# Expert gathers in float32 from one normed copy, one buffer of gathered tokens, a ring of 22 matrix buffers

## The chip, the core and the metric

The kernel runs on one core of a Trainium2 chip. TensorE (PE) multiplies matrices and loads their weights (PEld in the profile), VectorE (DVE), ScalarE (ACT) and GpSimd (POOL) do the elementwise work, and SyncE (SP) issues nearly all transfers from HBM to the on-chip memory, which 16 DMA engines carry out. Each engine has a queue of its own and runs it in order. The metric is the device time of one execution in microseconds. [...]

## The reference

Two transformer blocks are computed one after the other, on 256 tokens of 1024 features, in float32. The first has an attention mixer and a mixture of experts; the second a recurrent mixer and a dense feed-forward part. The change concerns the mixture of experts in the first block:

```python
def hierarchical_moe(h, w_group, b_group, w_router, b_router, w_gate, w_up, w_down):
    t = h.reshape(-1, d)
    g_logits = t @ w_group + b_group                 # 4 groups of 8 experts
    g_sel = jnp.argmax(g_logits, axis=-1)
    ...
    top_v, top_i = lax.top_k(e_logits, TOPK_EXPERT)  # 2 experts of the chosen group
    w_top = jax.nn.softmax(top_v, axis=-1) * p_group[:, None]
    comb = jnp.sum(jax.nn.one_hot(eid, N_EXPERTS) * w_top[..., None], axis=1)
    hg = jnp.einsum('nd,edf->nef', t, w_gate)        # 32 experts, 1024 x 256
    hu = jnp.einsum('nd,edf->nef', t, w_up)
    a = jax.nn.silu(hg) * hu * comb[:, :, None]
    y = jnp.einsum('nef,efd->nd', a, w_down)         # 32 experts, 256 x 1024
```

Each token goes to 2 of 32 experts. Three matrices of 1 MB belong to each expert, 96 MB in all, and each is read from HBM once.

## The kernel before

The experts are taken in 8 units of 4. A unit gives each of its experts 32 slots; a one-hot matrix tells which token sits in which slot. The unit's work on PE is, in the order of the loop at the end of the code below: gate product (`gate_up(st, "g")`, tile p_gu from the matrices eg), up product (p_gu from eu), then, for the next unit, `prepare`, which builds the one-hot matrix on DVE (`onehot`, tile Pq) and gathers that unit's tokens into its slots (`gather`: p_xg, moved into the tile xg by ACT and DVE, which also apply the norm's scale and shift), then `slots` (p_pw, the transposed one-hot matrix, and p_cs, each slot's weight in the mixture), `turn` (p_at, the activations transposed), `down` (p_dn from the matrices ed) and `scatter` (p_sc, which adds the result to the tokens).

The normed tokens are kept as three bf16 parts that add up to the float32 value (`xn3`, made by `cut3`; the trace calls them xn); so a gather is 3 parts x 2 token tiles x 8 feature tiles = 48 bf16 matmuls with a bf16 one-hot matrix. Unit 0's gather runs before the parts are there and is in float32 already (`gather_t`, tile P). The mixture weights are split in three bf16 columns too (`comb3`).

If an expert has more tokens than 32, the unit has a second set of slots. Ahead of units 1 to 6 stands `branch(st)`, a conditional block that does the whole unit again for the slots behind the 32nd, with a one-hot matrix and a gather of its own. Whether it runs is decided on the chip, by a count that each engine loads. For this input the block of unit 3 runs and the other five are skipped. The code of the block lies in the instruction stream in any case, and a skipped block is a jump. A hint for the branch stands on PE's queue, behind the `turn` of the unit before (`mark_branch_hint_location`). In unit 2's block there is also a fallback for counts above 64.

The expert matrices come through a ring of buffers of 1 MB in three pools (`RING`, `AGAIN`; pool 1 raw, 2 raw2, 3 raw3). `load_experts(n)` puts the next n loads on SP's queue: first 16, in front of the router 4 more, then 4 behind the gate, 4 (5 in unit 0) behind the up and 4 behind the down product of each unit. The fifth buffer of raw3 first holds the normed tokens in float32 (`xn2`) and serves as a buffer for matrices from then on, so that the first round of the ring has 20 places and each later one 21. A load waits until the matrix that its buffer held has been used. The instruction queues are put in order by a scheduler, from the order of the code, what each instruction depends on, and the calls that keep the order of the program.

There are two buffers for gathered tokens (`XGB = 2`), so that a second-slot unit gathers into one while the other keeps the tokens of the unit itself, which were gathered before the branch.

Of the kernel before, what the change touches and what calls it, by code (L numbers as in the profile page):

```python
# [17 lines left out]
D = 1024  # L18
# [3 lines left out]
SLOTS = 32  # L22
NEXP = 32
YF = 2
XGB = 2
RAW1 = 11
HALVES = ((0, 512), (512, 512))
LAST = ((0,512),(512,384),(896,128))


RING = [1, 1, 2, 2, 1, 1, 1, 1, 1, 2, 1, 1, 2, 2, 1, 1, 3, 3, 3, 3]
AGAIN = RING[:4] + [3] + RING[4:]


@with_exitstack
def tile_block(ctx: ExitStack, tc: tile.TileContext, A, out):
    nc = tc.nc
    pe, act, dve, pool = nc.tensor, nc.scalar, nc.vector, nc.gpsimd
# [10 lines left out]
    def bank(shape, name):  # L49
        return ps.tile(shape, FT, name=name, tag="bank")  # L50
# [51 lines left out]
    def mm(o, lhsT, rhs, start, stop):  # L102
        held_pe(pe.matmul(o, lhsT, rhs, start=start, stop=stop, skip_group_check=True))  # L103
# [127 lines left out]
    def load_experts(n):  # L231

        for _ in range(n):
            if not loads:
                return
            i = len(W)
            e, k = loads.pop(0)
            name = {"g": "w_gate", "u": "w_up", "d": "w_down"}[k]
            shape = (2, D) if k == "d" else (8, 256)
            n = RING[i] if i < len(RING) else AGAIN[(i - len(RING)) % len(AGAIN)]  # L240
            pool_, tag = (raw, "raw") if n == 1 else (raw2, "raw2") if n == 2 else (raw3, "raw3")
            t = pool_.tile([128, RAW], FT, name=f"e{k}", tag=tag)
# [13 lines left out]
            W[e, k] = v  # L256
# [631 lines left out]
    for c in "iiqikqqFqXFXbbYYbbvYTXXF22XY2XYvvYXYXv2BWBa2aaBYBnB3BC33CCCC3BCanB3C!CR4D45D45D45EH45DDDEoHEoEoDEoDEEESZpppp":  # L888
# [8 lines left out]
        else:  # L897
# [9 lines left out]


    m1 = p2.enter_context(tc.tile_pool(name="m1", bufs=1, side="right", reuse_waits="tile"))
    raw3 = p2.enter_context(tc.tile_pool(name="raw3", bufs=AGAIN.count(3), side="right", reuse_waits="tile"))  # L910

    xn2 = raw3.tile([128, RAW], FT, name="xn2", tag="raw3").rearrange("p (t d) -> p t d", t=2)
    tc.keep_in_program_order(pool.memset(xn2[:, 0, 0:1], 0.0))
    load_experts(RING.count(3))

    lg = m1.tile([128, 2, 36], FT, name="lg")
    le32 = m1.tile([128, 2, NEXP], FT, name="le32", tag="le32")
    iota1 = m1.tile([128, 2 * SLOTS], FT, name="iota1")
# [10 lines left out]
    gfi = m1.tile([128, 2], FT, name="gfi")  # L929
    top = m1.tile([128, 2, 8], FT, name="top")  # L930

    xn3 = m1.tile([128, 3, 2, 8, 128], BF, name="xn3")
    xh = [m1.tile([128, 8, 128], FT, name="h2", tag="xg", bufs=XGB).rearrange("p (a j) n -> p a j n", a=2),
          [m1.tile([128, 4, 128], FT, name="h2", tag="yf", bufs=YF) for _ in range(2)]]
    xh[0] = [xh[0][:, 0], xh[0][:, 1]]
    P0 = m1.tile([128, 2, 4, SLOTS], FT, name="P0", tag="sl")
    pos_ = bank([128, 2, NEXP], "p_pos")
    halves = [slice(0, 512), slice(512, 1024)]
    lgb = [None, None]
# [58 lines left out]
        held(dve.tensor_tensor(P0[:, t], iota1[:, None, 0:SLOTS].to_broadcast([128, 4, SLOTS]),  # L998
                               pos1[:, t, 0:4, None].to_broadcast([128, 4, SLOTS]), op=OP.is_equal))

    PP, XG = {}, {}
    P0f = P0.rearrange("p t e s -> p t (e s)")
    xgb = [bank([128, 4, 128], "p_xg") for _ in range(2)]

    def gather_t(t, js):
        for j in js:
            mm(xgb[j // 4][:, j % 4], xnj[:, t, j], P0f[:, t], t == 0 and j % 4 == 0, t == 1)

    def gather_mm(u, banks, t):
        for j in range(8):  # L1010
            for i in range(3):
                mm(banks[j // 4][:, j % 4], xn3[:, i, t, j], PP[u][:, t],
                   t == 0 and j % 4 == 0 and i == 0, t == 1 and i == 2)

    def cut3(src, parts, step):

        if step == 0:
            held(act.activation(parts[0], src, AF.Copy))
            held(dve.tensor_tensor(src, src, parts[0], op=OP.subtract))
        else:  # L1020
            held(act.activation(parts[1], src, AF.Copy))
            held(dve.tensor_tensor(parts[2], src, parts[1], op=OP.subtract))

    holding += [True, True]
    square(0, 0)
# [31 lines left out]

    def onehot(u, pos, slot):

        n = pos.shape[2]  # L1060
        P = m1.tile([128, 2, 4, SLOTS], BF, name="Pq", tag="Pq", bufs=3)[:, :, 0:n]
        for t in range(2):
            dve.tensor_tensor(P[:, t], slot[:, None, :].to_broadcast([128, n, SLOTS]),
                              pos[:, t, :, None].to_broadcast([128, n, SLOTS]), op=OP.is_equal)
        PP[u] = P.rearrange("p t e s -> p t (e s)")

    def gather(u, banks=None):

        n = 4 * SLOTS
        xg = m1.tile([128, 8, 128], FT, name="xg", tag="xg", bufs=XGB)[:, :, 0:n]  # L1070
        if not banks:
            banks = [bank([128, 4, 128], "p_xg")[:, :, 0:n] for _ in range(2)]
# [12 lines left out]
        XG[u] = xg  # L1085

    gather(0, xgb)

    for step in range(2):
        for t in range(2):  # L1090
            cut3(xnj[:, t], [xn3[:, i, t] for i in range(3)], step)
    del holding[:]
    onehot(0, pos1[:, :, 0:4], iota1[:, 0:SLOTS])


    p = bank([128, NEXP], "p_cnt")
# [19 lines left out]
    comb3 = m1.tile([128, 2, NEXP, 3], BF, name="comb3")  # L1116
    crest = m1.tile([128, 2, NEXP], FT, name="crest")
    dve.tensor_copy(comb3[:, :, :, 0], comb)
    dve.tensor_tensor(crest, comb, comb3[:, :, :, 0], op=OP.subtract)
    dve.tensor_copy(comb3[:, :, :, 1], crest)  # L1120
    dve.tensor_tensor(comb3[:, :, :, 2], crest, comb3[:, :, :, 1], op=OP.subtract)

    nu = len(ORDER)
# [16 lines left out]
    def gate_up(st, k):  # L1142
        if k == "g":
            st.b = bank([128, 512], "p_gu")
        o = 0 if k == "g" else 256
        for j in range(8):
            for c, e in enumerate(st.es):
                s0 = SLOTS * c
                mm(st.b[SLOTS * c:SLOTS * c + SLOTS, o:o + 256], XG[st.u][:, j, s0:s0 + SLOTS], W[e, k][:, j],
                   j == 0 and o == 0, j == 7)  # L1150

    def slots(st):

        P = PP[st.u]
        b = bank([128, 2, 128], "p_pw")
        for t in range(2):
            mm(b[:st.n, t], P[:, t], ident_b, t == 0, t == 1)
        st.PT = m1.tile([128, 2, 128], FT, name="PTs", tag="PTs", bufs=2)
        act.activation(st.PT[:st.n], b[:st.n], AF.Copy)
        b = bank([128, 3], "p_cs")  # L1160
        for t in range(2):
            for c, e in enumerate(st.es):
                s0 = SLOTS * c
                mm(b[SLOTS * c:SLOTS * c + SLOTS], P[:, t, s0:s0 + SLOTS], comb3[:, t, e], t == 0, t == 1)
        st.cs = m1.tile([128, 1], FT, name="cslot", bufs=2)
        dve.tensor_reduce(st.cs[:st.n], b[:st.n], axis=AX.X, op=OP.add)

    def silu(st):
        st.s = m1.tile([128, 256], FT, name="sl", tag="sl")
# [30 lines left out]
    def fallback():  # L1200
# [3 lines left out]
        with tc.If(rv > 2 * SLOTS):  # L1204
# [10 lines left out]
            for t in range(2):  # L1215
                banks = [bank([128, 4, 128], "p_tr") for _ in range(2)]
                for j in range(8):
                    for i in range(3):
                        mm(banks[j // 4][:, j % 4], xn3[:, i, t, j], ident_b, j % 4 == 0 and i == 0, i == 2)
                h2f = XG[NEXP + REST]  # L1220
# [86 lines left out]
    def branch(st):  # L1307

        rv = nc.values_load(cnti[0:1, st.u:st.u + 1])
        with tc.If(rv > SLOTS, label=f"more{st.u}"):  # L1310
# [19 lines left out]
    for k, st in enumerate(units):  # L1330
# [5 lines left out]
        gate_up(st, "g")  # L1336
        load_experts(n)
        gate_up(st, "u")
        load_experts(n + (k == 0))
        if k == 0:  # L1340
            gate_row_end()
            del holding[:]
# [623 lines left out]
```

## Time and profile before

| | us |
|---|---|
| median of 3 runs | 711.94 |
| lowest, highest | 711.85, 712.94 |
| the profiled execution | 711.57 |
| its span from the first to the last instruction | 709.3 |
| PE busy | 649.2 (92%) |
| DVE, ACT, POOL busy | 397.3, 301.2, 46.1 |

The span has 40 slices of 17.7 us on the page. The expert phase runs from about 192 us (the first gate product) to about 396 us; ahead of it lies the attention block, behind it the second block. In the rows below, a line of the timeline holds neighbouring instructions of one kind on one engine, x tells their number, and brackets hold how long the engine had been idle before and what released it. A float32 matmul leaves two records, a bf16 one leaves one. "issue" means that nothing shown was waited for; a name with q is an engine's sequencer, which runs branches.

### The profile page before, as it was taken

To read this page: it belongs to the slowest core of one execution; us is meant where nothing else is said; L and a number is where in the kernel's file an instruction comes from. 1 tells how busy PE (TensorE), PEld (TensorE's weight loads), DVE (VectorE), ACT (ScalarE), POOL (GpSimd) and SP (SyncE) were. 2 spreads that over 40 slices of the span, in tenths; PEclk is the share of its full clock that TensorE was granted. 3 is DMA by queue.
4 is the path that set the end of the run, shared out by engine and by line. 5 is a ranking of instruction groups with operands and counts; after the bars stand their busy time and mean duration, and the time that the engine had idled before them with its cause. 6 is when DMAs were issued, how large, how long until landed. Compare 5 with 4: busy or idle time off the path is not lost.

```text
span 709.3 us, 13260 instructions
## 1 busy us (share of the span) xinstructions
PE 649.2 (92%) x5475; PEld 503.5 (71%) x5475; DVE 397.3 (56%) x754; ACT 301.2 (42%) x505; POOL 46.1 (7%) x71
## 2 busy tenths in 40 slices
PE   4699999999897689987996999999999999999996
PEld 1398787777745244543453799978899999898994
DVE  2276977886661232322330689688575555555555
ACT  1456455553741011110111686856464444444445
POOL 7010000001000000000000613100000000000001
PEclk9789999999999899999999999999999999999998
DMA  9999579997599999999999997535355555550001
GB/s 341 369 374 391 210 304 328 309 420 308 239 373 418 418 417 418 406 420 417 418 421 382 383 363 298 171 119 178 119 185 203 197 188 178 178 179 1 1 1 59
DMA packets 69199, 196.89 MB, mean 278 GB/s; under 512 B 7550, under 2 KB 33219, under 8 KB 57350
## 3 DMA queue, kind: packets, MB, share of 16 engines
q1 hardware_dynamic: 67558, 195.30, 73.0%
q8 instruction: 50, 0.82, 0.5%
q10 hardware_dynamic: 1216, 0.30, 0.2%
q0 software_dynamic: 352, 0.28, 0.1%
q14 instruction: 23, 0.19, 0.1%
HBM read 194.81 MB, written 1.05 MB: 276 GB/s over the span
## 4 chain that ended last, share of the span: by engine, by line
PE 43%; DMA 6%; DVE 2%; ACT 1%; issue 0%; POOL 0%; ACTq 0%; POOLq 0%; DVEq 0%; SPq 0%
PE p_gu L103 20%; PE p_acc L103 11%; PE p_w L103 8%; DMA eu<-in_w_up_dram 3%; DMA ed<-in_w_down_dram 3%; PE p_dn L103 1%; PE p_o L103 1%; PE p_sc L103 1%; PE p_gate L103 0%; POOL xt L1799 0%; DVE w2l L90 0%; ACT SS L1802 0%; PE p_xg L103 0%; PE p_tr L1393 0%; PE p_row L103 0%
## 5 line engine op out<-in xcount | busy, mean ns | idle before, releaser
L103 PE MATMUL p_gu<-Xl,wguh 128*128 128x256 f32 x352 | 99.8, 284 | 0.0
L103 PE MATMUL p_gu<-Xh,wgul 128*128 128x256 f32 x352 | 99.3, 283 | 0.0
L103 PE MATMUL p_gu<-Xh,wguh 128*128 128x256 f32 x352 | 98.9, 283 | 0.1
L103 PEld LDWEIGHTS p_gu<-Xl,wguh 128*128 128x128 f32 x352 | 67.5, 192 | 0.5
L103 PEld LDWEIGHTS p_gu<-Xh,wguh 128*128 128x128 f32 x352 | 67.1, 192 | 0.7 <-ACT Xh L1395 0.4
L103 PEld LDWEIGHTS p_gu<-Xh,wgul 128*128 128x128 f32 x352 | 67.4, 192 | 0.3 <-DVE wgul L90 0.2
L103 PE MATMUL p_gu<-eg,xg 128*32 128x256 f32 x576 | 39.3, 426 | 18.5 <-PEq L1310 9.0
L1170 ACT ACTIVATE sl<-p_gu 128x256 f32<-128x256 f32 x9 | 3.5, 384 | 121.5 <-PE p_gu L103 121.5
L103 PEld LDWEIGHTS p_gu<-eg,xg 128*32 128x32 f32 x576 | 21.7, 122 | 37.0 <-issue 25.9
L90 DVE TENSOR_TENSOR wdnl<-wdn,wdnh 128x1024 fp32r<-128x1024 f32 x22 | 27.0, 1225 | 32.1 <-ACT wdnh L89 32.1
L103 PE MATMUL p_gu<-eu,xg 128*32 128x256 f32 x576 | 36.6, 391 | 5.1 <-DMA eu<-in_w_up_dram 5.0
L1171 DVE TENSOR_TENSOR sl<-sl,p_gu 128x256 f32<-128x256 f32 x9 | 3.8, 420 | 65.9 <-ACT sl L1170 65.9
L103 PE MATMUL p_w<-hTh,wih 128*128 128x256 f32 x128 | 37.9, 299 | 2.5 <-ACT wih L89 2.5
L90 DVE TENSOR_TENSOR wgul<-wup,wguh 128x1024 fp32r<-128x1024 f32 x22 | 26.9, 1225 | 21.6 <-ACT wguh L89 21.1
L89 ACT ACTIVATE wdnh<-wdn 128x1024 fp32r<-128x1024 f32 x22 | 23.3, 1058 | 36.2 <-PE p_gu L103 35.6
L103 PE MATMUL p_dn<-ed,aT 128*32 128x512 f32 (+2 forms) x304 | 33.7, 573 | 5.2 <-ACT aT L1178 5.2
L90 DVE TENSOR_TENSOR wgul<-wgt,wguh 128x1024 fp32r<-128x1024 f32 x22 | 27.0, 1225 | 19.8 <-ACT wguh L89 19.8
L89 ACT ACTIVATE wguh<-wgt 128x1024 fp32r<-128x1024 f32 x22 | 23.3, 1061 | 33.7 <-PE p_gu L103 18.2
L103 PE MATMUL p_w<-Xh,w2h 128*128 128x256 f32 x128 | 37.0, 289 | 0.5 <-ACT w2h L89 0.3
L103 PE MATMUL p_w<-hTl,wih 128*128 128x256 f32 x128 | 37.0, 290 | 0.0
L103 PE MATMUL p_w<-Xh,w2l 128*128 128x256 f32 x128 | 36.2, 284 | 0.6 <-DVE w2l L90 0.6
L103 PE MATMUL p_w<-hTh,wil 128*128 128x256 f32 x128 | 36.6, 291 | 0.0
(625 smaller groups left out, 1544.9 us busy)
## 6 DMA issues: line engine op xcount, KB each, us to landing
eg<-in_w_gate_dram SPq DMA_DIRECT2D x32, 1024.0 KB
eu<-in_w_up_dram SPq DMA_DIRECT2D x32, 1024.0 KB
ed<-in_w_down_dram SPq DMA_DIRECT2D x28, 1024.0 KB
wada<-in_w_ada_dram SPq DMA_DIRECT2D x24, 1024.0 KB
w<-in_w_in_dram SPq DMA_DIRECT2D x11, 1024.0 KB
wgt<-in_w_gate_up_dram SPq DMA_DIRECT2D x11, 1024.0 KB
wup<-in_w_gate_up_dram SPq DMA_DIRECT2D x11, 1024.0 KB
wdn<-in_w_down_dram SPq DMA_DIRECT2D x11, 1024.0 KB
```

Of the source, the lines that this page charges most:

```text
L89: held(act.activation(hi, src, AF.Copy))
L90: held(eng.tensor_tensor(lo, src, f32(hi), op=OP.subtract))
L103: held_pe(pe.matmul(o, lhsT, rhs, start=start, stop=stop, skip_group_check=True))
L1170: act.activation(st.s[:st.n], st.b[:st.n, 0:256], AF.Silu)
L1171: dve.tensor_tensor(st.s[:st.n], st.s[:st.n], st.b[:st.n, 256:512], op=OP.mult)
```

## The change

Seven things change, all in the expert phase.

1. The normed tokens stay in float32 only: `xn3`, `cut3`, `comb3` are gone. A gather is 2 x 8 = 16 float32 matmuls. p_pw is made from a float32 one-hot matrix with the float32 identity, p_cs from a float32 one-hot matrix and one column of `comb`, copied by DVE where it had been summed over three columns.
2. The one-hot matrices lie in two float32 tiles `hot[0]`, `hot[1]`, used in turn; unit 0's is the one with which its gather was done already, so it isn't built a second time.
3. There is one tile xg for gathered tokens. A second-slot unit overwrites it; so each conditional block ends with `gather(st.u)`, which gathers the unit's own tokens again.
4. xn2 is a tile of its own, and the write by POOL that held its buffer is gone.
5. The ring has 22 places in every round: raw3 has 6 buffers, all for matrices.
6. Six matrices rather than four are put on SP's queue in front of the router, and the up product of unit 0 is followed by 4 rather than 5.
7. The fallback (which doesn't run) takes its tokens from the float32 copy.

The core of the diff:

```diff
-RING = [1, 1, 2, 2, 1, 1, 1, 1, 1, 2, 1, 1, 2, 2, 1, 1, 3, 3, 3, 3]
-AGAIN = RING[:4] + [3] + RING[4:]
+RING = [1, 1, 2, 2, 1, 1, 1, 1, 1, 2, 1, 1, 2, 2, 1, 1, 3, 3, 3, 3, 3, 3]
...
-            n = RING[i] if i < len(RING) else AGAIN[(i - len(RING)) % len(AGAIN)]
+            n = RING[i % len(RING)]
...
-    raw3 = p2.enter_context(tc.tile_pool(name="raw3", bufs=AGAIN.count(3), side="right", reuse_waits="tile"))
-
-    xn2 = raw3.tile([128, RAW], FT, name="xn2", tag="raw3").rearrange("p (t d) -> p t d", t=2)
-    tc.keep_in_program_order(pool.memset(xn2[:, 0, 0:1], 0.0))
+    raw3 = p2.enter_context(tc.tile_pool(name="raw3", bufs=RING.count(3), side="right", reuse_waits="tile"))
     load_experts(RING.count(3))
+    xn2 = m1.tile([128, 2, D], FT, name="xn2")
...
-    xn3 = m1.tile([128, 3, 2, 8, 128], BF, name="xn3")
+    xg = m1.tile([128, 8, 128], FT, name="xg")
...
+    hot = [m1.tile([128, 2, 4, SLOTS], FT, name=f"hot{i}") for i in range(2)]
+    P0 = hot[0]
...
     def gather_mm(u, banks, t):
         for j in range(8):
-            for i in range(3):
-                mm(banks[j // 4][:, j % 4], xn3[:, i, t, j], PP[u][:, t],
-                   t == 0 and j % 4 == 0 and i == 0, t == 1 and i == 2)
+            mm(banks[j // 4][:, j % 4], xnj[:, t, j], PP[u][:, t], t == 0 and j % 4 == 0, t == 1)
...
-        P = m1.tile([128, 2, 4, SLOTS], BF, name="Pq", tag="Pq", bufs=3)[:, :, 0:n]
+        P = hot[(u + u // NEXP) % 2]
...
-        xg = m1.tile([128, 8, 128], FT, name="xg", tag="xg", bufs=XGB)[:, :, 0:n]
...
-    for step in range(2):
-        for t in range(2):
-            cut3(xnj[:, t], [xn3[:, i, t] for i in range(3)], step)
     del holding[:]
-    onehot(0, pos1[:, :, 0:4], iota1[:, 0:SLOTS])
...
-            mm(b[:st.n, t], P[:, t], ident_b, t == 0, t == 1)
+            mm(b[:st.n, t], P[:, t], ident, t == 0, t == 1)
...
-                mm(b[SLOTS * c:SLOTS * c + SLOTS], P[:, t, s0:s0 + SLOTS], comb3[:, t, e], t == 0, t == 1)
+                mm(b[SLOTS * c:SLOTS * c + SLOTS], P[:, t, s0:s0 + SLOTS], comb[:, t, e:e + 1], t == 0, t == 1)
...
-        dve.tensor_reduce(st.cs[:st.n], b[:st.n], axis=AX.X, op=OP.add)
+        dve.tensor_copy(st.cs[:st.n], b[:st.n])
...
             if st.u == REST:
                 fallback()
+            gather(st.u)
...
         gate_up(st, "u")
-        load_experts(n + (k == 0))
+        load_experts(n)
```

On PE, before, the end of unit 3's conditional block (its last products, then the branch) and the unit itself, up to the first matmuls of the next unit's gather:

```order
L1176 MATMUL p_at<-ident,sl 128x128 x2
L103 MATMUL p_dn<-ed,aT 32x512 x16
L103 MATMUL p_sc<-yf,PTs 128x512 x4
L1310 UNCONDITIONAL_BRANCH x2
L103 MATMUL p_gu<-eg,xg 32x256 x32
L103 MATMUL p_gu<-eu,xg 32x256 x32
L103 LDWEIGHTS xn_1908
L103 MATMUL p_xg<-Pq,xn_1908 128x128
```

And now, up to the turn of the unit:

```order
L1146 MATMUL p_at<-ident,sl 128x128 x2
L100 MATMUL p_dn<-ed,aT 32x512 x16
L100 MATMUL p_sc<-yf,PTs 128x512 x4
L100 MATMUL p_xg<-hot_1915,xn_1896 128x128 x16
L1279 UNCONDITIONAL_BRANCH x2
L100 MATMUL p_gu<-eg,xg 32x256 x32
L100 MATMUL p_gu<-eu,xg 32x256 x32
L100 MATMUL p_xg<-hot_1914,xn_1896 128x128 x16
L100 MATMUL p_pw<-ident,hot_1915 128x128 x2
L100 MATMUL p_cs<-le_1898,hot_1915 32x1 x8
L1146 MATMUL p_at<-ident,sl 128x128 x2
```

The block ends with a gather of 16 matmuls ahead of the branch, and the 48 matmuls of the next unit's gather (of which the first two stand above with their weight loads) are 16.

On SP, before, the loads of unit 1's four eu, its four ed and the first eg of unit 2, with the queues and engines that each waits for (DMAHW is the count of a transfer eight loads earlier):

```order
L255 DMA eu<-in_w_up_dram 128x2048 [waits DMAHW1_49,PE_49,Pool_49]
L255 DMA eu<-in_w_up_dram 128x2048 [waits DMAHW2_49]
L255 DMA eu<-in_w_up_dram 128x2048 [waits DMAHW3_49]
L255 DMA eu<-in_w_up_dram 128x2048 [waits DMAHW4_49]
L255 DMA ed<-in_w_down_dram 128x2048 [waits DMAHW5_49,PE_49]
L255 DMA ed<-in_w_down_dram 128x2048 [waits DMAHW6_49,PE_49]
L255 DMA ed<-in_w_down_dram 128x2048 [waits DMAHW7_49,PE_49]
L255 DMA ed<-in_w_down_dram 128x2048 [waits DMAHW0_49,PE_49]
L255 DMA eg<-in_w_gate_dram 128x2048 [waits DMAHW1_49,DVE_49,Pool_49]
```

And now:

```order
L252 DMA eu<-in_w_up_dram 128x2048 [waits DMAHW1_49,PE_49]
L252 DMA eu<-in_w_up_dram 128x2048 [waits DMAHW2_49]
L252 DMA eu<-in_w_up_dram 128x2048 [waits DMAHW3_49,PE_49,Pool_49]
L252 DMA eu<-in_w_up_dram 128x2048 [waits DMAHW4_49]
L252 DMA ed<-in_w_down_dram 128x2048 [waits DMAHW5_49]
L252 DMA ed<-in_w_down_dram 128x2048 [waits DMAHW6_49]
L252 DMA ed<-in_w_down_dram 128x2048 [waits DMAHW7_49,PE_49]
L252 DMA ed<-in_w_down_dram 128x2048 [waits DMAHW0_49,PE_49]
L252 DMA eg<-in_w_gate_dram 128x2048 [waits DMAHW1_49,PE_49]
```

Here the first two eu wait for one engine fewer and for an earlier instruction of PE, the third has PE and POOL, and the first two ed wait for no engine.

## Rows read from the trace of the kernel before

**Rows 1.** Busy time by stretch: us, busy us (x instructions) per engine, clock, DMA share, GB/s.
```profile
190.20:196.00 5.80, 5.80 (x92) 4.07 (x95) 4.50 (x22) 3.48 (x6) 0.00 (x0) 1.00 0.03 6
196.00:386.00 190.00, 159.23 (x1888) 85.49 (x1881) 57.94 (x116) 25.69 (x64) 1.02 (x2) 0.96 1.01 414
```

**Rows 2.** Timeline of SP, 174 to 200: start us, us, queue, line, transfer.
```profile
178.71 1.97 SPq L255 DMA_DIRECT2D eu<-in_w_up_dram  x4
195.57 1.99 SPq L255 DMA_DIRECT2D ed<-in_w_down_dram  x4
```

**Rows 3.** Chain of waits, end of the expert phase: start us, us, what.
```profile
341.72 19.71 DMA ed<-in_w_down_dram
...
361.49 19.91 DMA eu<-in_w_up_dram
...
381.44 5.08 PE p_gu L103 x58
```

**Rows 4.** Timeline of PE, unit 7: start us, us, instruction, [idle before <-releaser].
```profile
371.10 3.76 PE L103 MATMUL p_gu<-eg,xg 128*32 128x256 f32 x63
374.57 0.38 PE L103 MATMUL p_gu<-eu,xg 128*32 128x256 f32 x1
...
386.46 0.28 PE L103 MATMUL p_pw<-ident_b,Pq 128*128 128x128 bf16 x2
```

**Rows 5.** Busy time by stretch, from the end of unit 3's conditional block.
```profile
285.46:303.85 18.39, 17.80 (x229) 9.66 (x229) 6.70 (x14) 2.44 (x7) 0.00 (x0) 1.00 0.99 406
```

**Rows 6.** Timeline of PE, router and unit 0.
```profile
162.12 0.72 PE L103 MATMUL p_rb<-modcol,wr 128*36 128x1 f32 x16
...
189.94 2.03 PE L103 MATMUL p_xg<-P,xn 128*128 128x128 f32 x16
191.90 3.66 PE L103 MATMUL p_gu<-eg,xg 128*32 128x256 f32 x64
...
200.76 2.84 PE L103 MATMUL p_xg<-Pq,xn 128*128 128x128 bf16 x48
203.44 0.28 PE L103 MATMUL p_pw<-ident_b,Pq 128*128 128x128 bf16 x2
203.65 0.21 PE L103 MATMUL p_cs<-comb,Pq 128*32 128x3 bf16 x8
```

**Rows 7.** Timeline of PE, start of unit 3's conditional block.
```profile
265.57 2.85 PE L103 MATMUL p_xg<-Pq,xn 128*128 128x128 bf16 x48 [1.53 <-DVE Pq L1063]
```

**Rows 8.** Branch on PE's queue, units 1, 2, 4, 5, 6: ns min/median/max, first and last start.
```profile
L1310 PEldq COMPARE_BRANCH  x1: 6350/6350/6350, 210.1 to 210.1; - x1
L1310 PEldq COMPARE_BRANCH  x1: 1035/1035/1035, 234.7 to 234.7; - x1
L1310 PEldq COMPARE_BRANCH  x1: 846/846/846, 301.8 to 301.8; - x1
L1310 PEldq COMPARE_BRANCH  x1: 6129/6129/6129, 323.9 to 323.9; - x1
L1310 PEldq COMPARE_BRANCH  x1: 444/444/444, 348.8 to 348.8; - x1
```

**Rows 9.** Timeline of PE where it resumes after a branch.
```profile
216.84 1.70 PE L103 MATMUL p_gu<-eg,xg 128*32 128x256 f32 x16 [4.69 <-PEq L1310]
...
243.07 2.36 PE L103 MATMUL p_gu<-eg,xg 128*32 128x256 f32 x20 [6.09 <-DVEq L1310]
...
308.58 2.80 PE L103 MATMUL p_gu<-eg,xg 128*32 128x256 f32 x48 [1.81 <-issue]
...
330.46 4.98 PE L103 MATMUL p_gu<-eg,xg 128*32 128x256 f32 x64 [4.28 <-PEq L1310]
...
350.86 1.12 PE L103 MATMUL p_row<-modrow,ones 1*128 1x512 f32 x2
352.71 1.50 PE L103 MATMUL p_gu<-eg,xg 128*32 128x256 f32 x24 [0.73 <-ACTq L1310]
```

**Rows 10.** The page's DMA queues: packets, MB, share of 16 engines.
```profile
q8 instruction: 50, 0.82, 0.5%
```

More of the change, by code (lines that the diff above doesn't have):

```diff
@@ L24 @@
 YF = 2
-XGB = 2
 RAW1 = 11
@@ L930, in tile_block @@
     top = m1.tile([128, 2, 8], FT, name="top")
-    xn3 = m1.tile([128, 3, 2, 8, 128], BF, name="xn3")
-    xh = [m1.tile([128, 8, 128], FT, name="h2", tag="xg", bufs=XGB).rearrange("p (a j) n -> p a j n", a=2),
+    xg = m1.tile([128, 8, 128], FT, name="xg")
+    xh = [xg.rearrange("p (a j) n -> p a j n", a=2),
           [m1.tile([128, 4, 128], FT, name="h2", tag="yf", bufs=YF) for _ in range(2)]]
     xh[0] = [xh[0][:, 0], xh[0][:, 1]]
-    P0 = m1.tile([128, 2, 4, SLOTS], FT, name="P0", tag="sl")
+    hot = [m1.tile([128, 2, 4, SLOTS], FT, name=f"hot{i}") for i in range(2)]
+    P0 = hot[0]
     pos_ = bank([128, 2, NEXP], "p_pos")
@@ L999, in places @@
                                pos1[:, t, 0:4, None].to_broadcast([128, 4, SLOTS]), op=OP.is_equal))
-    PP, XG = {}, {}
-    P0f = P0.rearrange("p t e s -> p t (e s)")
+    PP = {0: P0.rearrange("p t e s -> p t (e s)")}
     xgb = [bank([128, 4, 128], "p_xg") for _ in range(2)]
@@ L1006, in gather_t @@
         for j in js:
-            mm(xgb[j // 4][:, j % 4], xnj[:, t, j], P0f[:, t], t == 0 and j % 4 == 0, t == 1)
+            mm(xgb[j // 4][:, j % 4], xnj[:, t, j], PP[0][:, t], t == 0 and j % 4 == 0, t == 1)
     def gather_mm(u, banks, t):
         for j in range(8):
-            for i in range(3):
-                mm(banks[j // 4][:, j % 4], xn3[:, i, t, j], PP[u][:, t],
-                   t == 0 and j % 4 == 0 and i == 0, t == 1 and i == 2)
[L1015 to L1022, printed above, removed]
+            mm(banks[j // 4][:, j % 4], xnj[:, t, j], PP[u][:, t], t == 0 and j % 4 == 0, t == 1)
     holding += [True, True]
@@ L1058, in onehot @@
     def onehot(u, pos, slot):
-        n = pos.shape[2]
-        P = m1.tile([128, 2, 4, SLOTS], BF, name="Pq", tag="Pq", bufs=3)[:, :, 0:n]
+        P = hot[(u + u // NEXP) % 2]
         for t in range(2):
-            dve.tensor_tensor(P[:, t], slot[:, None, :].to_broadcast([128, n, SLOTS]),
-                              pos[:, t, :, None].to_broadcast([128, n, SLOTS]), op=OP.is_equal)
+            dve.tensor_tensor(P[:, t], slot[:, None, :].to_broadcast([128, 4, SLOTS]),
+                              pos[:, t, :, None].to_broadcast([128, 4, SLOTS]), op=OP.is_equal)
         PP[u] = P.rearrange("p t e s -> p t (e s)")
     def gather(u, banks=None):
-        n = 4 * SLOTS
-        xg = m1.tile([128, 8, 128], FT, name="xg", tag="xg", bufs=XGB)[:, :, 0:n]
         if not banks:
-            banks = [bank([128, 4, 128], "p_xg")[:, :, 0:n] for _ in range(2)]
+            banks = [bank([128, 4, 128], "p_xg") for _ in range(2)]
             for t in range(2):
@@ L1084, in gather @@
                                            op0=OP.mult, op1=OP.add))
-        XG[u] = xg
     gather(0, xgb)
-    for step in range(2):
-        for t in range(2):
-            cut3(xnj[:, t], [xn3[:, i, t] for i in range(3)], step)
     del holding[:]
-    onehot(0, pos1[:, :, 0:4], iota1[:, 0:SLOTS])
     p = bank([128, NEXP], "p_cnt")
@@ L1115, in tile_block @@
         dve.scalar_tensor_tensor(comb[:, t], comb[:, t], w1[:, t:t + 1], selb[:, t], op0=OP.mult, op1=OP.mult)
[L1116 to L1121, printed above, removed]
     nu = len(ORDER)
@@ L1148, in gate_up @@
                 s0 = SLOTS * c
-                mm(st.b[SLOTS * c:SLOTS * c + SLOTS, o:o + 256], XG[st.u][:, j, s0:s0 + SLOTS], W[e, k][:, j],
+                mm(st.b[SLOTS * c:SLOTS * c + SLOTS, o:o + 256], xg[:, j, s0:s0 + SLOTS], W[e, k][:, j],
                    j == 0 and o == 0, j == 7)
@@ L1156, in slots @@
         for t in range(2):
-            mm(b[:st.n, t], P[:, t], ident_b, t == 0, t == 1)
+            mm(b[:st.n, t], P[:, t], ident, t == 0, t == 1)
         st.PT = m1.tile([128, 2, 128], FT, name="PTs", tag="PTs", bufs=2)
         act.activation(st.PT[:st.n], b[:st.n], AF.Copy)
-        b = bank([128, 3], "p_cs")
+        b = bank([128, 1], "p_cs")
         for t in range(2):
@@ L1217, in fallback @@
                 for j in range(8):
-                    for i in range(3):
-                        mm(banks[j // 4][:, j % 4], xn3[:, i, t, j], ident_b, j % 4 == 0 and i == 0, i == 2)
-                h2f = XG[NEXP + REST]
+                    pe.transpose(banks[j // 4][:, j % 4], xnj[:, t, j], ident)
+                h2f = xg
                 for j in range(8):
```

## The prediction

> **What bounds the kernel now.** I read the busy shares by stretch first, then the chain of waits, then TensorE's timeline through the expert phase, and last the rows of the branch instruction. From 196 to 386 us the DMA engines are at a share of 1.01 with 414 GB/s, while TensorE (PE) is busy 159.23 of 190 us [rows 1]: the 76 matrices that are still to come arrive one behind the other. Before that they stand still, at a share of 0.03 for 5.8 us, until SP issues four ed at 195.57 [rows 1, 2]. The chain says the same: it runs through the transfers of ed (19.71 us) and eu (19.91 us) and ends on an eu that frees PE at 381.44 [rows 3]. In unit 7 PE has its gate product done from 371.10 to 374.57, in 3.47 us, and ends the equally long up product only at 386.46 [rows 4]. Without the transfers PE would have been there at 374.57 + 3.47 = 378.04. So **PE has a slack of 386.46 − 378.04 = 8.4 us at the end of the phase**, and it is a slack of the whole phase: whatever PE does longer from 190 us on is added up and set against it once. Behind unit 7 the chain is PE again to the end of the program.
>
> A unit without a branch's cost takes PE 18.39 us, busy for 17.80 [rows 5]. It is never idle there but for the turn of silu.
>
> **Memory: two more matrices early.** Before, SP issues four eu at 178.71 and then waits until 195.57 for gate products of unit 0 to free slots [rows 2]; the DMA engines run dry at 190.2. Afterwards, by the order of SP, the first two eu wait for an earlier out-projection matmul, and two ed need no slot freed at all. They move in the gap: 2 MB at 414 GB/s are 5.0 us, and the stretch without transfers has 5.8. So the stream of transfers would end 5.0 us earlier, at 381.5. This is a gain only if PE is not later than that.
>
> **PE: the gathers.** A gather was 48 bf16 matmuls, 200.76 to 203.44 = 2.68 us. Now it is 16 in float32, of 128x128 each. Unit 0 already had such a gather: 16 records (8 matmuls) take 1.96 us until the next tile starts, of which about 0.17 is the start; records follow each other at 0.1117 us, that is 0.223 a matmul, and 16 are 3.57 us [rows 6]; from below twice 1.96 less three starts, 3.41, from above 3.92. So **+0.89 per gather**. The two p_pw were 0.21 us [rows 6] and become 4 records of 0.1117 = 0.45: +0.24. The eight p_cs took 0.21 us; their nearest row in float32 with one column is p_rb, 16 records in 0.72 us but with 36 columns of weights, 128 partitions and one output group, where p_cs writes four groups of 32 rows. The bounds are 0 and +0.51; I take +0.2, as the four groups are nearer to the lower one. Per unit +1.33 (bounds 0.7 and 2.0), on PE's own stream with nothing beside it, since matmuls wait for PE alone. Units 0 to 6 do a gather for the next: **7 × 1.33 = 9.3**. What leaves ACT and DVE (the bf16 cuts, the reduction over three columns) stands beside the gates of unit 0 and is worth nothing there: ACT and DVE are far from full.
>
> **PE: the branch that is taken.** Of the six conditional blocks one runs, that of unit 3 (from 265.57 to 285.46 [rows 5, 7]). It grows by a gather's 0.89, by 0.44 for p_pw and p_cs, and by the second gather of the unit at its end, 3.57 and about 0.2 for the evictions that the gate must now wait for, since there is one buffer: **+5.1**. The other five pay nothing for it in work, but in code.
>
> **PE: where the code lies.** A block that is skipped costs PE a jump, and two prices stand in the trace. The branch took 6350 ns for unit 1 and 6129 ns for unit 5, but 846 and 444 ns for units 4 and 6, and 1035 for unit 2 [rows 8]. PE's matmuls resumed with idles of 4.69 and 4.28 us in the dear cases and 0.73 in unit 6, behind a p_row of 1.12 (unit 2's 6.09 us end on DVE's jump) [rows 9]. [...]
> [...]
> [...]
> [...]
> [...]
> [...] After such an idle the 64 records of unit 5's gate ran 4.98 us, where the 63 of unit 7's took 3.76 [rows 9, 4]: +1.2. [...]
>
> [...]
>
> **The sum.** PE's lag at the end of unit 7's up product: 9.3 + 5.1 + 0.9 − 1.8 − 0.5 + 7.7 = 20.7 us. The slack is 8.4, so the end moves by 12.3; the transfers, now done at 381.5, are no longer waited for. In the tail p_pw and p_cs add 0.4. The 58 records behind the last transfer took 5.08 us [rows 3], slow for the same reason as a gate behind an idle; a little of that slowness must reach into the down product, and I estimate 0.7 won back there, half of what such a gate loses: +12.0. The profiled execution took 711.57 us (0.37 under the median): 711.57 + 12.0 = **723.6, said as 724**.
>
> **Rivals.**
> [...]
> [...]
> Third, on the other side: the transfers stay the bound, and the two early matrices decide. 711.57 − 5.0 = 706.6. It holds if PE's lag stays below 8.4 − 5.0 = 3.4 us. The gathers alone cost 9.3, so float32 matmuls would have to be hidden under weight loads, and the second gather under the jump. Against it: PE's records of unit 0's gather follow each other without a hole.
> Fourth, both meet: a lag of 7 to 9.8 us, which needs gathers at their lower bound, unit 6 cheap and unit 4's stop gone: 7 × 0.7 + 5.1 − 1.8 = 8.2. No change.
>
> **How the numbers follow.** Forecast 0.52, first rival 0.23, second 0.13, fourth 0.05, third 0.07. The forecast's own range, from the bounds of p_cs and of the jumps, is 719 to 728. From 713 to 731 it takes in the first two rivals with their bounds. About 0.2% (1.4 us) is what can be told from no change. Faster 0.07, same 0.05, slower 0.88.
>
> **What would show it.** In the new profile: p_xg with 32 records in about 3.57 us in each unit, twice in unit 3; no wait of p_gu for an eu transfer in unit 7; a DMA share that drops below 1 before the phase ends; the branch of unit 6 at some 6 us and a stop early in that gate; no stop in unit 4's gate; transfers going on between 190 and 196. The forecast is wrong if unit 7's up product still waits for transfers, or if unit 6's branch takes under 1 us.

## The result and the profile after

| | before | after |
|---|---|---|
| median us | 711.99 (15 runs) | 717.40 (15 runs) |
| lowest, highest | 711.12, 712.96 | 713.04, 720.04 |
| profiled execution | 711.57 | 713.04 |
| its span | 709.3 | 711.3 |
| PE, PEld busy in it | 649.2, 503.5 | 659.1, 516.6 |

The ratio is 1.0069 with an interval from 1.005 to 1.0087. The change makes the kernel 5.4 us slower, where the prediction said 12: the direction was right and the size less than half of it. The changed kernel also spreads over 7 us where the kernel before keeps within 1.9, and the profiled execution is its fastest. So its trace shows the best case, and three more executions were profiled for that reason (again1 to again3, below).

The windows view of the changed kernel, by stretch (us; PE, PEld, DVE, ACT, POOL busy; TensorE's granted clock as a share of full speed, DMA share, GB/s), answers to [rows 1]:

```profile
190.00:196.00 6.00, 6.00 (x105) 3.87 (x107) 2.08 (x9) 3.00 (x5) 0.00 (x0) 1.00 0.52 175
285.00:290.00 5.00, 5.00 (x35) 4.01 (x34) 2.50 (x5) 0.00 (x0) 0.00 (x0) 1.00 0.27 113
290.00:295.30 5.30, 5.30 (x93) 2.97 (x95) 1.57 (x6) 1.72 (x4) 0.00 (x0) 1.00 0.10 17
```

The first row is what the ring gave: a share of 0.52 where it was 0.03. The other two are what it did not save: from about 286 to 295 us the transfers stand almost still. This hole is the new thing in the trace. SP's timeline shows why (it answers to [rows 2]):

```profile
178.91 16.41 SPq L252 DMA_DIRECT2D ed<-in_w_down_dram  x4
...
265.23 30.00 SPq L252 DMA_DIRECT2D ed<-in_w_down_dram  x4
...
294.26 0.97 SPq L252 DMA_DIRECT2D ed<-in_w_down_dram  x2
295.32 3.20 SPq L252 DMA_DIRECT2D eg<-in_w_gate_dram  x4
```

Of the four ed from 265.23 on (the first row for them joins all four) the last two go out at 294.26 only: SP waits 22.8 us for a place in the ring, until unit 3's gate product has used its eg, which it has at 294.25. That product comes behind the conditional block that is taken. Timeline of PE there (start us, us, instruction, idle before; answers to [rows 6, 7]):

```profile
199.72 3.73 PE L100 MATMUL p_xg<-hot,xn 128*128 128x128 f32 x32
203.28 0.61 PE L100 MATMUL p_pw<-ident,hot 128*128 128x128 f32 x4
203.82 0.31 PE L100 MATMUL p_cs<-le,hot 128*32 128x1 f32 x16
204.06 0.51 PE L1146 MATMUL p_at<-ident,sl 128*128 128x128 f32 x2
...
265.50 3.81 PE L100 MATMUL p_xg<-hot,xn 128*128 128x128 f32 x32 [1.63 <-DVE hot L1048]
...
286.74 3.73 PE L100 MATMUL p_xg<-hot,xn 128*128 128x128 f32 x32
290.41 3.84 PE L100 MATMUL p_gu<-eg,xg 128*32 128x256 f32 x64
```

From the first gather of the block to the unit's own gate it is 290.41 − 265.50 = 24.9 us, where it was 19.9 before. And at the end of the phase the chain (start us, us, what) still runs through transfers [rows 3], and PE still waits for them in unit 7 [rows 4]:

```profile
363.70 20.01 DMA eu<-in_w_up_dram
...
383.73 9.61 DMA ed<-in_w_down_dram
...
393.39 1.48 PE p_dn L100 x10
```

```profile
376.65 3.66 PE L100 MATMUL p_gu<-eg,xg 128*32 128x256 f32 x64
380.13 1.36 PE L100 MATMUL p_gu<-eu,xg 128*32 128x256 f32 x6
383.76 3.64 PE L100 MATMUL p_gu<-eu,xg 128*32 128x256 f32 x58 [2.27 <-DMA eu<-in_w_up_dram]
```

The prediction had PE as the bound here and no wait. The down product (p_dn) now waits for the last ed as well, which comes later than the last eu.

The reading that follows is a simple one. Once the ring has run dry in unit 3's block, the rest of the phase is a fixed train of transfers that starts when unit 3's gate product ends. So the time of an execution should be the end of that product plus a constant. Worked out for each profiled execution (end of the gate product, its start and length added; the execution's time; their difference):

| kernel | ring | gate of unit 3 ends | time | difference |
|---|---|---|---|---|
| before | 21 | 289.12 | 711.57 | 422.45 |
| before_long | 21 | 295.37 | 717.36 | 421.99 |
| ring21 | 21 | 300.60 | 722.82 | 422.22 |
| after | 22 | 294.25 | 713.04 | 418.79 |
| again1, again2, again3 | 22 | 300.14, 301.09, 298.57 | 718.54, 719.44, 716.94 | 418.40, 418.35, 418.37 |
| light_early | 22 | 291.02 | 709.46 | 418.44 |
| light_late | 22 | 294.04 | 712.70 | 418.66 |
| yf_hint_warm | 22 | 290.40 | 709.06 | 418.66 |
| yf_hint_warm_dve | 22 | 288.47 | 706.88 | 418.41 |
| before_light | 21 | 283.21 | 710.49 | 427.28 |

Over some 12 us of difference in the gate's end the constant holds within 0.5 us in the rows of either ring, before_light apart. Worked out in the same way, hint_late, yf_xg and hint_warm have 418.5, 419.1 and 419.4 and before_hint has 422.7, so over all of them it holds within 1.1 us (22 places) and 0.7 us (21); in hint_warm, the largest, unit 7's up product waits for no transfer. Only before_light leaves it, and it has no hole in its transfers.

### The profile page after: what moved, and what is told of

It reads as the page before. It is cut to its first block, busy times and chain, and to the rows that moved or that the text cites. A ratio compares the mean times of both kernels' runs of the same rounds, so it can differ in the third digit from the quotient of the medians.

```text
span 711.3 us, 13279 instructions
## 1 busy us (share of the span) xinstructions
PE 659.1 (93%) x5469; PEld 516.6 (73%) x5469; DVE 394.9 (56%) x748; ACT 299.8 (42%) x505; POOL 48.8 (7%) x70
## 5 line engine op out<-in xcount | busy, mean ns | idle before, releaser
L100 PE MATMUL p_gu<-eg,xg 128*32 128x256 f32 x576 | 37.2, 401 | 11.5 <-DVEq L1279 8.4
L100 PEld LDWEIGHTS p_xg<-hot,xn 128*128 128x128 f32 x320 | 38.1, 197 | 5.7 <-issue 4.3
L100 PE MATMUL p_xg<-hot,xn 128*128 128x128 f32 x320 | 39.9, 284 | 1.8 <-DVE hot L1048 1.6
L100 PEld LDWEIGHTS p_gu<-eg,xg 128*32 128x32 f32 x576 | 19.7, 115 | 29.3 <-issue 15.2
L100 PE MATMUL p_w<-Xl,w2h 128*128 128x256 f32 x128 | 36.3, 285 | 1.2 <-DVE Xl L1367 1.1
L1063 ACT ACTIVATE xg<-p_xg,modcol,af 128x128 f32<-128x128 f32 x40 | 17.3, 459 | 47.7 <-DVE xg L1066 47.5
L100 PE MATMUL p_gu<-eu,xg 128*32 128x256 f32 x576 | 34.8, 379 | 2.4 <-DMA eu<-in_w_up_dram 2.3
```

## The experiments

Theory: the changed kernel's end is set by how late unit 3's gate product ends, because the ring starves in the taken block. Rival: what the prediction said, PE's total lag less one slack at the end. The two differ on where a saving of PE counts. The edits that follow are cut to their core.

**light_early and light_late.** One edit, in three units ahead of unit 3 or in three behind it; it leaves out three quarters of the columns of most of the up product, and so 7 us of PE:

```diff
-                mm(st.b[..., o:o + 256], xg[:, j, s0:s0 + SLOTS], W[e, k][:, j], j == 0 and o == 0, j == 7)
+                n = 64 if k == "u" and st.u in (0, 1, 2) and j else 256      # light_late: (4, 5, 6)
+                mm(st.b[..., o:o + n], xg[:, j, s0:s0 + SLOTS], W[e, k][:, j, 0:n], j == 0 and o == 0, j == 7)
```

Expected of light_early: 

> The changed kernel, but in the up products of units 0, 1 and 2 seven of eight feature tiles multiply 64 instead of 256 columns (part of the product is left out): 3.57 x 7/8 x 3/4 = 2.3 us less of PE per unit, 7.0 in all, ahead of unit 3; instructions, loads and order are the same. Theory (the ring starves while the taken branch runs: the end of the phase is the end of unit 3's gate product plus the time of the 38 matrices that are then still to come, about 99 us): the starved time falls from some 9.3 to 2.3 us and the kernel is 7 us faster than the changed kernel in like executions, a median near 710.5. Rival (PE is the bound at the end, as predicted): also 7 us faster; this run alone doesn't tell them apart, its twin in units 4 to 6 does.

Expected of light_late: 

> The same shortening (part of the product is left out) in units 4, 5 and 6 instead, 7.0 us less of PE behind unit 3. Theory (ring starved in the taken branch, then transfers bound the end): no change against the changed kernel beyond about 1 us, a median of 716.5 to 717.5, and the wait for the transfers of eu in unit 7 grows by about 7 us. Rival (PE bounds the end, as predicted): 5 to 7 us faster, a median near 711.

Measured: light_early 708.36 (ratio to before 0.9948, 0.9925 to 0.9972), light_late 716.94 (1.0064, 1.0039 to 1.0089). The same 7 us of PE are worth 9 ahead of unit 3 and 0.5, nothing that can be told, behind it. The rival falls. (That light_early won 2 us more than it leaves out may come from the branch of unit 1, below, which took 1502 ns in its profiled execution; what it took in the others is not known.) In light_late the saved time turns into waits of unit 7, for eg already and then for eu, 5.8 us in all where the changed kernel waited 2.27 us. The wait was expected to grow by about 7 us and grew by 3.5; most of the rest went into the 58 records behind it, 6.21 us where the changed kernel's took 3.64. Timeline of PE in light_late:

```profile
373.18 3.42 PE L100 MATMUL p_gu<-eg,xg 128*32 128x256 f32 x57 [1.82 <-DMA eg<-in_w_gate_dram]
...
378.16 0.62 PE L100 MATMUL p_gu<-eu,xg 128*32 128x256 f32 x2 [1.33 <-DMA eu<-in_w_up_dram]
380.67 0.62 PE L100 MATMUL p_gu<-eu,xg 128*32 128x256 f32 x2 [1.90 <-DMA eu<-in_w_up_dram]
383.20 6.21 PE L100 MATMUL p_gu<-eu,xg 128*32 128x256 f32 x58 [0.75 <-DMA eu<-in_w_up_dram]
```

**before_long and before_light.** The same question put to the kernel before: a longer block, and less PE ahead of it.

```diff
+            if st.u == 3:                                   # before_long, at the end of the conditional block
+                for _ in range(2):
+                    banks = [bank([128, 4, 128], "p_xg") for _ in range(2)]
+                    for t in range(2):
+                        gather_mm(x.u, banks, t)
```

(before_light has the edit of light_early, on the kernel before.)

Expected of before_long: 

> The kernel before, with two more passes of the gather's 48 matmuls at the end of unit 3's conditional block only (their result is not used): 2 x 2.68 = 5.4 us more of PE there. Theory (the taken block is where the ring runs out; in the kernel before its transfers get through it with a slack of 1 to 2 us): 3.5 to 4.5 us slower, 715.5 to 716.5. Rival (the prediction's step: PE has one slack of 8.4 us for the whole phase, set against its lag at the end): no change, 711.6 to 712.4.

Expected of before_light: 

> The kernel before with the shortening of light_early: in the up products of units 0, 1 and 2 seven of eight feature tiles multiply 64 instead of 256 columns (part of the product is left out), 7.0 us less of PE ahead of unit 3; order, loads and hints are the same. Theory (in the kernel before the transfers are busy throughout, and the ring runs out just as unit 3's gate ends): no change, 711 to 712, where the changed kernel won 9 us by the same edit. Rival 1 (the kernel before too ends a constant after unit 3's gate): 705. Rival 2 (part of PE's work ahead of unit 3 counts, because the ring starves a little): 708 to 710.

Measured: before_long 717.02 (1.007, 1.0055 to 1.0085), that is 5.1 us slower for 5.5 us of matmuls; before_light 711.71 (1.0, 0.9989 to 1.001). So the slack of 8.4 us was of no use to unit 3's block; there the kernel before had almost none, less than I gave it in the expectation too (1 to 2 us). And what is saved ahead of the block gives it nothing either, as the transfers are busy throughout: it stood on the corner of both bounds. The block in before_long, timeline of PE:

```profile
286.25 5.52 PE L103 MATMUL p_xg<-Pq,xn 128*128 128x128 bf16 x96
291.71 3.66 PE L103 MATMUL p_gu<-eg,xg 128*32 128x256 f32 x64
```

Its transfers in the same place, and those of before_light (windows view):

```profile
290.00:296.00 6.00, 6.00 (x112) 4.23 (x113) 0.00 (x0) 0.00 (x0) 0.00 (x0) 1.00 0.20 81
```

```profile
280.00:296.00 16.00, 15.41 (x220) 8.81 (x213) 4.83 (x12) 2.44 (x7) 0.00 (x0) 1.00 1.01 419
```

**ring21.** The changed kernel with one place fewer.

```diff
-RING = [1, 1, 2, 2, 1, 1, 1, 1, 1, 2, 1, 1, 2, 2, 1, 1, 3, 3, 3, 3, 3, 3]
+RING = [1, 1, 2, 2, 1, 1, 1, 1, 1, 2, 1, 1, 2, 2, 1, 1, 3, 3, 3, 3, 3]
```

> The changed kernel with 21 instead of 22 places in the ring (one raw3 buffer fewer, five instead of six matrices ahead of the router). Theory (end = end of unit 3's gate product + the matrices still to come): 39 instead of 38 are to come, 2.5 us slower than the changed kernel: median 719.9, best 715.5. Rival (PE bounds the end): no change, 717.4.

Measured: 720.93 (1.0129, 1.0111 to 1.0147), 3.5 us slower than the changed kernel. The direction is the theory's, the size is not: one matrix is 2.5 us, and by the table above a place is worth 3.8 (422.2 against 418.4). The expected best execution of 715.5 did not come either: the fastest took 720.08. The traces, one execution each, show where the other 1.3 us lie. The last eu comes 392.60 − 300.60 = 92.0 us after the gate's end in ring21 and 387.85 − 298.57 = 89.3 in again3; that is 2.7, one matrix. The 58 records behind it then took 6.56 us, at a granted clock of 0.55, instead of 3.64 at 1.00, so that PE no longer waits for ed and starts the scatter 0.7 us later still; the last 0.4 us fall behind that. Timeline of PE, ring21 and then again3:

```profile
392.60 6.56 PE L100 MATMUL p_gu<-eu,xg 128*32 128x256 f32 x58 [1.90 <-DMA eu<-in_w_up_dram]
...
404.21 1.99 PE L100 MATMUL p_sc<-yf,PTs 128*128 128x512 f32 x4
```

```profile
387.85 3.64 PE L100 MATMUL p_gu<-eu,xg 128*32 128x256 f32 x58 [2.07 <-DMA eu<-in_w_up_dram]
...
398.75 1.98 PE L100 MATMUL p_sc<-yf,PTs 128*128 128x512 f32 x4
```

**yf_xg.** No second gather: the second-slot unit's tokens go to buffers that are free until its down product.

```diff
+        to = [xg[:, j] for j in range(8)]
+        if u >= NEXP:
+            yx = [m1.tile([128, 4, 128], FT, name="xg2", tag="yf", bufs=YF) for _ in range(2)]
+            to = [yx[j // 4][:, j % 4] for j in range(8)]
+        XG[u] = to
...
-            gather(st.u)
```

> The changed kernel without the second gather at the end of each conditional block: a second-slot unit gathers into two halves that share the buffers of yf, which are idle until its down product; the unit's own tokens stay in xg. PE has 3.7 us less in unit 3's block, and each skipped block is 64 instructions shorter. Theory (ring starved in the taken branch): the end moves by the same 3.7 to 3.9 us: median near 713.5, the best executions near 709.3, faster than the kernel before. Rival (PE bound): the same 3.7 us. If the cost of the change came from neither, but from the matmul price of the gathers alone, nothing: 717.

Measured: 713.88 (1.0019, 1.0001 to 1.0037), lowest 708.55: 3.5 us of the changed kernel's 5.4 are the second gather. Its profiled execution lost the hint of unit 1 as again3 below did (a hint is called lost here where its branch took over 5 us; this one took 7021 ns), and started unit 0 within 0.2 us of it; unit 3's gate ended 3.85 us earlier (294.72 against 298.57).

**hint_late and hint_warm.** The branch hint 4 down matmuls later; then also more warming matmuls in the router.

```diff
-            with tc.issue_after(st.turned):           # behind the turn
+            with tc.issue_after(st.mid):              # behind the first 4 of 16 down matmuls
                 tc.mark_branch_hint_location(f"more{k + 1}", "LikelyTaken", [mybir.EngineType.PE])
...
-    warm(1)                                           # hint_warm only
+    warm(7)
     experts(0)
```

Expected of hint_late: 

> The changed kernel with the branch hint moved from behind the turn to behind the first 4 of the 16 down matmuls, about 1.9 us later on PE's queue. [...] Rival 1 (the spread has another cause): the spread from 713 to 720 stays and the median is 717. [...]

Expected of hint_warm: 

> The changed kernel with the later hint of hint_late and, in the router, 7 instead of 1 warming matmuls ahead of the second p_lg, where PE otherwise idles 1.49 us and the 16 records of p_lg then take 1.98 us in some executions and 3.26 to 3.49 in others. Theory (the changed kernel's spread from 713 to 720 is made of two events ahead of unit 3, the lost hint of unit 1 at some 4 us and the slow clock behind this idle at some 1.5 to 2.5 us, and both reach the end because the ring starves in unit 3's block): median 713, all runs within 712 to 714.5. Rival (the spread comes from the transfers): median 716 to 717 and a spread of 3 us or more, as in hint_late.

Measured: hint_late 716.67 (1.007, 1.0052 to 1.0087), from 715.45 to 718.54; hint_warm 715.77 (1.0057, 1.0036 to 1.0078), from 713.53 to 718.38. hint_late was expected near 713, with 1.5 to 3 us for the branch of unit 1, and hint_warm at 713; both times were missed. The steps happened: that branch took 1782 and 1057 ns in the profiled executions, and p_lg 1.97 us in hint_warm. But hint_late's profiled execution, its fastest, ran p_lg in 3.49 us and started unit 0 2.6 us later than the changed kernel's (193.42 against 190.85), and in hint_warm the later hint is lost in other places: the branches of units 2 and 4 took 5922 and 6140 ns. What the slower executions of these two kernels spent was not seen.

**again1 to again3.** The changed kernel itself.

Expected of again1: 

> The changed kernel once more, to see an execution other than the fastest. In every execution so far of a kernel with a ring of 22 the time is 418.4 to 419.4 us after the end of unit 3's gate product. Theory: this one keeps to that, and if it is slower than 714 its unit 3 is later for one of two reasons that the trace shows: the branch of unit 1 costs over 5 us (the hint ran before the instruction packet that was under way began to move), or unit 0 starts later than 192 us (slow clock in the router). Rival: unit 3's gate ends at 294 as in the profiled execution and the time is lost behind it, in the transfers.

Expected of again2: 

> As again1: time = end of unit 3's gate product + 418.4 to 419.4 us; over 714 only with a branch of unit 1 over 5 us or a start of unit 0 behind 192 us. Rival: lost behind unit 3.

Expected of again3: 

> As again1: time = end of unit 3's gate product + 418.4 to 419.4 us; over 714 only with a branch of unit 1 over 5 us or a start of unit 0 behind 192 us. Rival: lost behind unit 3.

Measured: 718.54, 719.44, 716.94. All three lose the hint of unit 1, and all keep to the constant, so nothing is lost behind unit 3. Branch of unit 1 on PE's queue (ns min/median/max, start), the fastest execution first, then the three, each in a fence of its own:

```profile
L1279 PEldq COMPARE_BRANCH  x1: 1657/1657/1657, 210.5 to 210.5; - x1
```

```profile
L1279 PEldq COMPARE_BRANCH  x1: 6101/6101/6101, 212.6 to 212.6; - x1
```

```profile
L1279 PEldq COMPARE_BRANCH  x1: 6326/6326/6326, 213.5 to 213.5; - x1
```

```profile
L1279 PEldq COMPARE_BRANCH  x1: 6886/6886/6886, 210.6 to 210.6; - x1
```

In again1 and again2 the router's second p_lg (the product that gives the routing logits) is slow besides, 3.63 and 3.58 us. Timeline of PE, again2 and then again3:

```profile
183.92 3.58 PE L100 MATMUL p_lg<-wr,h 128*128 128x36 f32 x16 [1.50 <-DVE h L962]
...
193.79 3.66 PE L100 MATMUL p_gu<-eg,xg 128*32 128x256 f32 x64
...
220.11 6.08 PE L100 MATMUL p_gu<-eg,xg 128*32 128x256 f32 x64 [4.56 <-PEq L1279]
```

```profile
182.52 1.98 PE L100 MATMUL p_lg<-wr,h 128*128 128x36 f32 x16 [1.50 <-DVE h L962]
...
190.89 3.66 PE L100 MATMUL p_gu<-eg,xg 128*32 128x256 f32 x64
...
217.78 6.07 PE L100 MATMUL p_gu<-eg,xg 128*32 128x256 f32 x64 [5.12 <-PEq L1279]
```

So in these four executions the spread of the changed kernel is made ahead of unit 3: 4.3 us by the hint (unit 3's gate of again3 against the fastest execution, at the same start of unit 0), up to 3 by where unit 0 starts. The kernel before has the lost hint in its profile too; that it doesn't show in its time, because its transfers were busy, is what before_light suggests (its gate of unit 3 ended 5.9 us earlier for nothing), but no run shows it with the hint itself.

**before_hint.** The kernel before, hint behind 8 of 16 down matmuls (the edit of hint_late, four matmuls further on).

> The kernel before, with the branch hint moved behind the first 8 of 16 down matmuls, some 2.5 us later on PE's queue, so that it runs when the instruction packet under way has moved: the branches of units 1 and 5 should take 1 to 3 us instead of 6.1 to 6.4, and unit 3's gate ends 3 to 4 us earlier. Theory (in the kernel before two bounds meet in unit 3's block: the transfers are busy throughout and the ring runs out just as the gate ends, at a slack under 0.5 us): nothing is won, 711 to 712, since the transfers were never idle. Rival 1 (the law that the time is the end of unit 3's gate plus a constant holds for earlier ends too): 708 to 709. Rival 2 (the prediction's slack of 8.4 us of PE at the end): 711.6 to 712.2, as in the theory; the kernel with the longer block has told those two apart.

Measured: 711.85 (1.0003, 0.9988 to 1.0018). It did not reach its condition: the branches of units 1, 5 and 6 took 6182, 5879 and 5986 ns. So it says nothing on what a hint that works would be worth; before_light took its place.

**yf_hint_warm and yf_hint_warm_dve.** All of it together: no second gather, later hint, warming; and a hint for DVE's jump of unit 2.

```diff
+            if k == 1:                                      # yf_hint_warm_dve only
+                with tc.issue_after(st.scaled):             # behind DVE's scaling of the down product
+                    tc.mark_branch_hint_location("more2", "LikelyTaken", [mybir.EngineType.DVE])
```

Expected of yf_hint_warm_dve: 

> The changed kernel without the second gather (as in yf_xg), with the later hint, 7 warming matmuls and a hint for the branch of unit 2 on DVE's queue too, behind the second scaling of unit 1. Theory: 3.7 us less in unit 3's block and some 5 us less at unit 2, where PE waits 6.3 us for DVE's jump; both ahead of unit 3's gate, and the ring starves 9 us there in the changed kernel: 713 - 3.7 - 5 = 704.3, or 706.6 if the transfers then bind throughout; some 6 us faster than the kernel before. If DVE's hint does nothing: 709.3. Rival (PE at the end or spread from transfers): 712 or more.

Expected of yf_hint_warm: 

> The version without the second gather, with the later hint and the warming, but without the hint on DVE's queue. Theory: against the version with it (707.2) PE waits again some 6 us for DVE's jump at unit 2, of which all but the little that the transfers then bind comes back: 711 to 712.5, about the kernel before. If the DVE hint was worth nothing: 707.

Measured: 707.23 (0.9940, 0.9925 to 0.9954) and 707.40 (0.9934, 0.9918 to 0.9950): 4.7 and 4.4 us faster than the kernel before, and within 1.2 and 2.6 us from lowest to highest. The first expectation named about 704 to 707, and 707.2 came, but not for its reason: the hint on DVE's queue did nothing. PE waits as long without it as with it (timeline of PE, unit 2, without and with):

```profile
241.07 6.14 PE L100 MATMUL p_gu<-eg,xg 128*32 128x256 f32 x64 [6.38 <-DVEq L1291]
```

```profile
239.92 2.36 PE L100 MATMUL p_gu<-eg,xg 128*32 128x256 f32 x20 [6.33 <-DVEq L1293]
```

The second expectation, 711 to 712.5, was wrong with it; its other branch, 707 if DVE's hint was worth nothing, is what came. Against the changed kernel the two win some 10 us, about what the second gather (3.5), the hint of unit 1 (4.3) and the start of unit 0 (up to 3) add up to above; how they share it was not tried, and the hint and the warming alone won 1.6 (hint_warm).

## Why the prediction was wrong in size

**The gathers: right.** 203.28 − 199.72 = 3.56 us for the 16 matmuls (predicted 3.57), p_pw 0.54 (0.45), p_cs 0.24 (0.41), together 204.06 − 199.72 = 4.34 against 203.79 − 200.76 = 3.03 before: +1.31 per unit, predicted +1.33. That the sum fits so closely is in part luck, as the two small terms miss in opposite directions. Before:

```profile
203.79 0.50 PE L1176 MATMUL p_at<-ident,sl 128*128 128x128 f32 x2
```

**The taken block: right.** 24.9 against 19.9 us: +5.0, predicted +5.1.

**The two early matrices: right as a step.** SP issued two ed at 178.9 and the share between 190 and 196 us rose to 0.52. (The four eu ahead of them went out 3 us earlier too, at 175.75 instead of 178.71, so the two did not all fall into that gap.)

**The code's place: wrong.** The sum has four terms for branches, worked out from where hints and branches lie in the program: +0.9 (unit 1), −1.8 (the stop at 308.58 in unit 4's gate product [rows 9], taken to go), −0.5 (unit 5) and +7.7 (unit 6, taken to become dear). That the place sets such costs no run shows. What the runs show in its place: the stop in unit 4 did go (the gate's 64 records run 3.66 us from 312.42 without a break), but units 1, 5 and 6, which the author took to be dear or nearly so, took 1657, 1249 and 420 ns in the changed kernel's profile. In again1 to again3 the same program at the same places took over 6 us for unit 1, so it is not the place that decides. What the traces show instead stands in the last section. For unit 6, the term of +7.7, nothing came: 420 ns in each of the four executions. Without it, the first rival's case, the sum is 711.57 + 12.0 − 7.7 = 715.9, the nearer number; but it counts with the same slack as the forecast, so that it came within 1.5 us of the median is luck. Both signs that the prediction named for being wrong are there: this branch under 1 us, and an up product of unit 7 that waits for transfers (2.27 us).

**The failed step is the slack.** The prediction says "it is a slack of the whole phase: whatever PE does longer from 190 us on is added up and set against it once", and then "the transfers, now done at 381.5, are no longer waited for". (381.5 is the end of the up product, 386.46, less 5.0; the last eu came at 381.44 before, so 5.0 earlier is 376.4. It came at 383.76.) light_late shows the first false (7 us less PE behind unit 3, no change), before_long too (5.5 us more in unit 3's block of the kernel before, 5.1 slower, although the end had 8.4 us). The transfers can't run ahead by more than the ring holds. A block of 20 to 25 us, behind which the next eg come free, is as long as 8 to 10 matrices at 2.5 us (1 MB at 414 GB/s); the ring was just large enough for it before, at a DMA share of 0.95 between 285 and 290 us, and ran dry for some 9 us with the longer one, in the fastest execution. Windows view of the kernel before:

```profile
285.00:290.00 5.00, 5.00 (x86) 2.76 (x88) 1.49 (x4) 0.00 (x0) 0.00 (x0) 1.00 0.95 397
```

From there on the train of transfers is late by a fixed amount, and PE has slack again behind it. So the lag does not have to be added up to the end of unit 7, but to unit 3's gate, and there the ring's 22nd place is set against it. With constants from other executions: the gate's end of again3, whose time is near the median, is 298.57 − 289.12 = 9.45 us later than before; the constant is 418.4 (again1, again2) instead of 422.2 (ring21), 3.8 less; 9.45 − 3.8 = 5.6, where 716.94 − 711.57 = 5.4 was measured.

**The third rival** (the transfers stay the bound) had the right engine at the end, and the wrong sign, since it took their stream for unbroken.

**The spread: not foreseen.** Over the four executions of the changed kernel the branch of unit 1 took 1657 to 6886 ns and the router's second p_lg 1.98 to 3.63 us; the one trace of the kernel before shows one outcome, 6350 ns and 1.98 us, and there, as before_light suggests, the transfers hid what it cost.

## What to carry to other kernels

Slack that a chain shows at the end of a streamed phase is not slack of its middle: for each long stretch in which no buffer comes free, compare its length with what the ring can load in it, and add up the delays only to the end of the longest one. Where the ring does run dry there and the compute engine has room behind it, work is best taken out ahead of its end and can be left behind it; where it doesn't run dry, as in before_light, work taken out ahead won nothing either. And if executions of a changed kernel spread more than those of the kernel before, look at several traces before explaining one.

## What the runs showed of the hardware

**In these traces a branch hint was lost, nearly always, where another instruction packet began to move within 2.8 us behind it.** Times from the traces: the hint on PE's queue, the packet of the instruction queue nearest to it (0.82 MB in 50 packets, 16 KB each [rows 10]), and the branch's cost, for unit 1:

| kernel | hint at us | packet starts | branch ns |
|---|---|---|---|
| before | 203.13 | 1.54 us after | 6350 |
| again1 | 205.90 | 0.46 after | 6101 |
| again2 | 206.79 | 0.39 after | 6326 |
| before_hint | 204.63 | 0.34 after | 6182 |
| again3 | 203.90 | 0.18 after | 6886 |
| light_early | 204.27 | 0.03 after | 1502 |
| after | 203.85 | 0.22 before | 1657 |
| light_late | 204.63 | 0.25 before | 1662 |
| hint_late | 207.92 | 1.44 before | 1782 |

Over the 80 skipped branches in 16 traces, a packet began 0.03 to 2.8 us after the hint in 18, and 16 of these were dear (5.9 to 7.0 us); the two that were not are unit 1 of light_early (0.03) and unit 5 of before_light (0.31). In the other 62 the next packet began 3.5 us or more after the hint, and one was dear (unit 5 of before_hint, 5879 ns). The 63 that were not dear took 0.4 to 2.0 us. No run forced the order by itself, so this is read from the traces alone, with three exceptions of 80, and why a hint is lost they don't show.

**The same 8 matmuls (16 records of p_lg) took 1.98 or 3.26 to 3.63 us behind the same idle of 1.5 us.** The granted clock of the stretch from 184 to 188 us was 1.00 in light_late, where p_lg took 1.98, and 0.50 in hint_late, where it took 3.49. Which of the two times came differed from kernel to kernel and from execution to execution. In hint_warm and yf_hint_warm, where six more warming matmuls keep PE busy through that idle (1.73 us of p_warm in hint_warm), p_lg took 1.97 and 1.98 us.
